# Three time steps per partition, Exp in place, and a first store in two parts: prefix log-sum-exp on one core

## The chip, the cores and the metric

The kernel runs on one NeuronCore of a Trainium2 chip. The metric is the device time of one execution in microseconds; lower is better. The kernel before takes 1265.46 us (median of 10 runs, 1264.6 to 1266.16).

## The reference

`x` is float32 of shape (4, 4096, 4128): four sequences of 4096 time steps, 4128 columns each. The output is the running log-sum-exp along time, kept per column:

```
out[:, 0, :] = x[:, 0, :]
for t in range(1, S):
    mx = np.maximum(out[:, t - 1, :], x[:, t, :])
    out[:, t, :] = mx + np.log(np.exp(out[:, t - 1, :] - mx) + np.exp(x[:, t, :] - mx))
```

This is the log of a prefix sum of exp(x), and that is how the kernel works: Exp, a prefix sum over time by matrix multiplication, Ln. 270.53 MB are read and 270.53 MB written.

## The kernel before

A tile holds 256 consecutive time steps of one sequence, all 4128 columns: partition p holds the R = 2 steps 2p and 2p+1, which lie side by side in DRAM, so a partition's run is 33,024 bytes. Tiles live in `xpool` (5 buffers). There are 64 of them, 16 per sequence, worked through in order of time.

The columns of a tile are taken in four chunks of 1024; a tail of 32 columns rides along with the last one. For a chunk, ScalarE writes Exp of both rows as fp16 into a buffer `et` (L111, four buffers). TensorE then forms the prefix sum in PSUM (`pt`, three buffers of two banks): `incl`, a triangle of ones with its diagonal, times the first rows, plus `excl`, the triangle without it, times the second rows, plus `pick` times the carry of the tile before (`head`). That is the sum up to each partition's first row; Ln of it goes into row 0 of the tile in place (L126). TensorE then adds `ident` times the second rows (`second`), and Ln of the result goes into row 1 (`close`). VectorE takes the last partitions of `pt` as the carry, as an fp16 value and an fp16 remainder (`keep`, L90 and L91). The tail has a small PSUM tile `qt` of its own and one Ln for both rows (L149).

Inside a tile the chunks are staggered by hand in `run`: while the Exp of chunk c is issued, row 0 of chunk c-1 and row 1 of chunk c-2 are finished. At the end of a tile everything drains before the next tile's first Exp.

Order of the transfers: all loads (L102) and stores (L153) are issued by the SP queue, in program order. Four loads are issued at the start; then comes, for each tile i, the load of tile i+3 (where there is one not yet issued) and the store of tile i. From tile 5 on a load reuses the buffer of an earlier tile and waits on SP until that tile's store has landed; the stores behind it wait as well. The instruction orders of the engines are fixed by the program (a manual schedule); a layer under it derives the semaphore waits from which tiles and columns each instruction reads and writes.

Of the kernel before, what the change touches and what calls it, by code (L numbers as in the profile page):

```python
# [7 lines left out]
FP32 = mybir.dt.float32  # L8
FP16 = mybir.dt.float16
ACT = mybir.ActivationFunctionType  # L10
P = 128
R = 2
CH = 1024
MM = 512
HI, LO = 96, 32
# [2 lines left out]
def _constants(nc, pool):  # L18


    def tri(base, name):
        t = pool.tile([P, P], FP16, name=name)
        nc.gpsimd.memset(t, 1.0)

        nc.gpsimd.affine_select(  # L25
            out=t, in_=t, pattern=[[1, P]], compare_op=mybir.AluOpType.is_ge,
            fill=0.0, base=base, channel_multiplier=-1,
        )
        return t

    def ones_where_zero(bases, step, name):
        t = pool.tile([P, P], FP16, name=name)
        nc.gpsimd.memset(t, 0.0)
        for base in bases:
            nc.gpsimd.affine_select(  # L35
                out=t, in_=t, pattern=[[step, P]], compare_op=mybir.AluOpType.not_equal,
                fill=1.0, base=base, channel_multiplier=1,
            )
        return t

    return (
        tri(0, "incl"),
        tri(-1, "excl"),
        ones_where_zero([0], -1, "ident"),
        ones_where_zero([-(HI + 31), -(LO + 31)], 0, "pick"),
    )


@with_exitstack
def kernel(  # L50
    ctx: ExitStack,
    tc: tile.TileContext,
    x: bass.AP,
    out: bass.AP,
):

    nc = tc.nc
    B, S, D = x.shape  # L60
    rows = P * R
    n_t = S // rows
    assert S % rows == 0
    n_main = D // CH
    tail = D - n_main * CH
    t0 = n_main * CH

    nc.scalar.preload_act_table_set("natural_log_exp_and_others")  # L68
    consts = ctx.enter_context(tc.tile_pool(name="consts", bufs=1))
    incl, excl, ident, pick = _constants(nc, consts)  # L70

    xpool = ctx.enter_context(tc.tile_pool(name="xpool", bufs=5))
    epool = ctx.enter_context(tc.tile_pool(name="epool", bufs=4))
    cpool = ctx.enter_context(tc.tile_pool(name="cpool", bufs=1))
    pmain = ctx.enter_context(tc.tile_pool(name="pmain", bufs=3, space=bass.MemoryType.PSUM))
    ptail = ctx.enter_context(tc.tile_pool(name="ptail", bufs=2, space=bass.MemoryType.PSUM))

    carry = [cpool.tile([P, CH], FP16, name=f"carry{c}") for c in range(n_main)]
    carry_t = cpool.tile([P, tail], FP16, name="carry_t")
    for t in (*carry, carry_t):  # L80
        nc.vector.memset(t, 0.0)  # L81

    ctx.enter_context(tc.manual_schedule())

    def mm(pt, w, rhs, start, stop):
        nc.tensor.matmul(pt, lhsT=w, rhs=rhs, start=start, stop=stop, skip_group_check=True)  # L86

    def keep(cr, pt):

        nc.vector.tensor_copy(cr[HI:HI + 32, :], pt[HI:HI + 32])  # L90
        nc.vector.tensor_tensor(  # L91
            out=cr[LO:LO + 32, :], in0=pt[HI:HI + 32], in1=cr[HI:HI + 32, :],
            op=mybir.AluOpType.subtract,
        )

    class Step:
        def __init__(self, b, k):
            self.first = k == 0
            self.xt = xpool.tile([P, R, D], FP32, name="xt")
            self.et, self.pt = {}, {}  # L100
            self.dram = lambda t: t[b, k * rows:(k + 1) * rows, :].rearrange("(p j) d -> p j d", j=R)
            nc.sync.dma_start(out=self.xt, in_=self.dram(x))  # L102

        def cols(self, c):
            return slice(c * CH, (c + 1) * CH if c + 1 < n_main else D)

        def exp(self, c):
            s = self.cols(c)
            w = s.stop - s.start
            et = epool.tile([P, R, CH + tail], FP16, name="et")  # L110
            nc.scalar.activation(et[:, :, :w], self.xt[:, :, s], ACT.Exp)  # L111
            self.et[c] = et

        def head(self, c):
            et = self.et[c]
            pt = self.pt[c] = pmain.tile([P, CH], FP32, name="pt")
            for s in range(0, CH, MM):
                mm(pt[:, s:s + MM], incl, et[:, 0, s:s + MM], True, False)
            for s in range(0, CH, MM):
                mm(pt[:, s:s + MM], excl, et[:, 1, s:s + MM], False, self.first)  # L120
            if not self.first:
                for s in range(0, CH, MM):
                    mm(pt[:, s:s + MM], pick, carry[c][:, s:s + MM], False, True)

        def ln(self, j, c):
            nc.scalar.activation(self.xt[:, j, c * CH:(c + 1) * CH], self.pt[c], ACT.Ln)  # L126

        def second(self, c):
            pt = self.pt[c]
            for s in range(0, CH, MM):  # L130
                mm(pt[:, s:s + MM], ident, self.et[c][:, 1, s:s + MM], False, True)

        def close(self, c):

            self.ln(1, c)
            keep(carry[c], self.pt[c])

        def tail_mm(self):
            et = self.et[n_main - 1]
            qt = self.qt = ptail.tile([P, R, tail], FP32, name="qt")  # L140
            e0, e1 = et[:, 0, CH:], et[:, 1, CH:]
            for j in range(R):
                mm(qt[:, j, :], incl, e0, j == 0, False)
                mm(qt[:, j, :], incl if j else excl, e1, False, self.first)
                if not self.first:
                    mm(qt[:, j, :], pick, carry_t, False, True)

        def ln_tail(self):
            nc.scalar.activation(self.xt[:, :, t0:D], self.qt, ACT.Ln)  # L149
            keep(carry_t, self.qt[:, 1, :])  # L150

        def store(self):
            nc.sync.dma_start(out=self.dram(out), in_=self.xt)  # L153

        def run(self):
            last = n_main - 1
            self.exp(0)
            self.head(0)
            for c in range(1, n_main):
                self.exp(c)  # L160
                self.head(c)
                if c == last:
                    self.tail_mm()
                self.ln(0, c - 1)
                self.second(c - 1)
                if c >= 2:
                    self.close(c - 2)
            self.ln(0, last)
            self.second(last)
            self.close(last - 1)  # L170
            self.ln_tail()
            self.close(last)
            self.store()

    work = [(b, k) for b in range(B) for k in range(n_t)]
    ahead = 3
    steps = []
    for i, (b, k) in enumerate(work):
        if i == 0:
            steps += [Step(*work[n]) for n in range(ahead)]  # L180
        if i + ahead < len(work):
            n = i + ahead
            steps.append(Step(*work[n]))
        steps[i].run()


# [28 lines left out]
```

The softmax here doesn't subtract the row's maximum and nothing guards it: scores larger than these inputs give would overflow.

## Time and profile before

| | |
|---|---|
| median of 10 runs | 1265.46 us |
| the profiled execution | 1264.59 us, span 1262.9 us |
| DMA queue of SP | 18,432 packets, busy 99.5% of 16 engines' span |
| ScalarE busy | 963.4 us (76%) |
| TensorE busy, weight loads | 667.4 us (53%), 242.4 us (19%) |
| VectorE busy | 655.8 us (52%) |
| load, from issue to landing | median 29.4 us |
| store, from issue to landing | median 38.6 us |
| one Ln of 128 x 1024 | 1028 ns |
| one Exp of 128 x 2048 | 1903 ns |

The share of a row is its busy time over the span of the profiled execution. A transfer of 4,128 KB runs on 16 DMA engines, eight descriptors (one per partition) and a completion on each. The time from issue to landing is longer than the transfer itself, because earlier transfers stand ahead of it on the same engines. The trace also keeps a record of each packet on the DMA engines, with its queue, size, start and duration; the queues 8 and 14 in it fetch instructions.

### The profile page before, as it was taken

How to read it: one execution, taken by the hardware profiler on the slowest of the kernel's cores; microseconds unless marked ns; L12 is line 12 of the kernel's file. 1: busy time of each engine (PE TensorE's matmuls, PEld its weight loads, DVE VectorE, ACT ScalarE, POOL GpSimd, SP SyncE). 2: the span in 40 equal slices, each digit the busy share in tenths (PEclk: the TensorE clock that was granted, in tenths of full speed). 3: DMA queues.
4: the chain of work that ended last, by engine and by line, in shares of the span. 5: the costliest groups of instructions: out<-in, count | busy, mean ns of one | idle time of the engine just before them, and what ended most of it. 6: DMA issues, size and time to landing. Idle time of an engine off the chain costs nothing.

```text
span 1262.9 us, 7025 instructions
## 1 busy us (share of the span) xinstructions
PE 667.4 (53%) x2392; PEld 242.4 (19%) x2392; DVE 655.8 (52%) x645; ACT 963.4 (76%) x833; POOL 2.2 (0%) x13
## 2 busy tenths in 40 slices
PE   2665655535455454554554555546545555455551
PEld 1222221212112121121111221212112121121220
DVE  3556655464454544545546455464564544645443
ACT  5888878778678787787877877777778777787772
POOL 0000000000000000000000000000000000000000
PEclk9778778787777777777777778767687677877776
DMA  9999999999999999999999999999999999999997
GB/s 402 417 433 429 433 430 434 429 431 432 434 430 434 433 431 432 432 434 433 434 430 433 432 434 433 434 433 431 433 432 431 432 434 434 433 434 434 431 433 335
DMA packets 18466, 541.51 MB, mean 429 GB/s; under 512 B 2048, under 2 KB 2048, under 8 KB 2048
## 3 DMA queue, kind: packets, MB, share of 16 engines
q1 hardware_dynamic: 18432, 541.07, 99.5%
q8 instruction: 19, 0.31, 0.1%
q14 instruction: 15, 0.12, 0.0%
HBM read 270.53 MB, written 270.53 MB: 428 GB/s over the span
## 4 chain that ended last, share of the span: by engine, by line
DMA 88%; ACT 1%; PE 1%; SPq 1%; DVE 1%; issue 0%; ACTq 0%
DMA out_dram<-xt 83%; DMA xt<-in_x_dram 5%; PE pt L86 1%; SPq L102 1%; ACT xt L126 1%; ACT et L111 0%; DVE carry L90 0%; DVE carry L91 0%; SPq L153 0%; DVE carry_t L90 0%; DVE carry_t L91 0%; ACTq L126 0%
## 5 line engine op out<-in xcount | busy, mean ns | idle before, releaser
L90 DVE CAST carry<-pt 32x1024 f16<-32x1024 f32 x256 | 314.9, 1230 | 574.1 <-ACT xt L126 570.8
L126 ACT ACTIVATE xt<-pt 128x1024 f32<-128x1024 f32 x512 | 504.4, 1028 | 126.1 <-PE pt L86 65.3
L111 ACT ACTIVATE et<-xt 128x2048 f16<-128x2048 f32 (+1 forms) x256 | 485.4, 1920 | 149.3 <-DMA xt<-in_x_dram 149.3
L86 PE MATMUL pt<-et,incl 128*128 128x512 f16 x512 | 211.0, 504 | 546.1 <-ACT et L111 373.7
L91 DVE TENSOR_TENSOR carry<-pt,carry 32x1024 f16<-32x1024 f32 x256 | 314.0, 1226 | 8.8
L86 PE MATMUL pt<-et,excl 128*128 128x512 f16 x512 | 211.6, 505 | 0.0
L86 PEld LDWEIGHTS <-incl 128*128 128x128 f16 x704 | 69.2, 111 | 683.8 <-issue 640.6
L86 PE MATMUL pt<-carry,pick 128*128 128x512 f16 x480 | 194.9, 497 | 0.0
L86 PE MATMUL pt<-et,ident 128*128 128x512 f16 x512 | 178.3, 435 | 24.8 <-ACT xt L126 24.8
L86 PEld LDWEIGHTS <-excl 128*128 128x128 f16 x576 | 71.3, 124 | 116.6 <-issue 84.7
L86 PEld LDWEIGHTS <-pick 128*128 128x128 f16 x600 | 69.5, 118 | 94.7 <-issue 66.9
L86 PEld LDWEIGHTS <-ident 128*128 128x128 f16 x512 | 49.4, 106 | 100.3 <-issue 73.7
L86 PE MATMUL qt<-et,incl 128*128 128x32 f16 x192 | 20.0, 192 | 0.0
L86 PE MATMUL qt<-carry_t,pick 128*128 128x32 f16 x120 | 15.6, 182 | 0.0
L149 ACT ACTIVATE xt<-qt 128x64 f32<-128x64 f32 x64 | 14.5, 227 | 0.0
L90 DVE CAST carry_t<-qt 32x32 f16<-32x32 f32 x64 | 12.6, 197 | 2.0
L91 DVE TENSOR_TENSOR carry_t<-qt,carry_t 32x32 f16<-32x32 f32 x64 | 12.4, 193 | 2.2
L86 PE MATMUL qt<-et,excl 128*128 128x32 f16 x64 | 11.7, 183 | 0.0
L81 DVE MEMSET carry<- 128x512 uint32 x4 | 1.9, 485 | 1.1 <-PEq L199 1.0
L68 ACT ACT_TABLE_LOAD x1 | 1.3, 1283 | 0.8 <-PEq L199 0.8
L35 POOL TENSOR_SCALAR_AFFINE_SELECT pick<-pick 128x128 f16<-128x128 f16 x2 | 0.6, 292 | 0.1
L25 POOL TENSOR_SCALAR_AFFINE_SELECT excl<-excl 128x128 f16<-128x128 f16 x1 | 0.3, 293 | 0.0
(11 smaller groups left out, 1.9 us busy)
## 6 DMA issues: line engine op xcount, KB each, us to landing
xt<-in_x_dram SPq DMA_DIRECT2D x64, 4128.0 KB, 29.4
out_dram<-xt SPq DMA_DIRECT2D x64, 4128.0 KB, 38.6
```

Source lines behind the costliest of these rows:

```text
L25: nc.gpsimd.affine_select(out=t, in_=t, pattern=[[1, P]], compare_op=mybir.AluOpType.is_ge, fill=0.0, base=base, channel_multiplier=-1,)
L35: nc.gpsimd.affine_select(out=t, in_=t, pattern=[[step, P]], compare_op=mybir.AluOpType.not_equal, fill=1.0, base=base, channel_multiplier=1,)
L68: nc.scalar.preload_act_table_set("natural_log_exp_and_others")
L81: nc.vector.memset(t, 0.0)
L86: nc.tensor.matmul(pt, lhsT=w, rhs=rhs, start=start, stop=stop, skip_group_check=True)
L90: nc.vector.tensor_copy(cr[HI:HI + 32, :], pt[HI:HI + 32])
L91: nc.vector.tensor_tensor(out=cr[LO:LO + 32, :], in0=pt[HI:HI + 32], in1=cr[HI:HI + 32, :], op=mybir.AluOpType.subtract,)
L102: nc.sync.dma_start(out=self.xt, in_=self.dram(x))
L111: nc.scalar.activation(et[:, :, :w], self.xt[:, :, s], ACT.Exp)
L126: nc.scalar.activation(self.xt[:, j, c * CH:(c + 1) * CH], self.pt[c], ACT.Ln)
L149: nc.scalar.activation(self.xt[:, :, t0:D], self.qt, ACT.Ln)
```

## The change

R becomes 3: partition p of a tile holds three consecutive time steps, 49,536 bytes. 4096 steps are 32 blocks of 128, so a sequence has ten tiles of three rows and one of two; in the first sequence the two-row tile comes first, in the others last. There are 44 tiles, and `xpool` has four buffers of three-row size. Matrix products go on as before with one more stage: after row 0, `ident` times the next row is added twice.

There is no `et` buffer. The tile is also seen as fp16 (`half`), and Exp writes its fp16 result over the first half of the bytes of the same columns; the Ln of a row later overwrites them with float32.

The chunks of all tiles form one stream. In pass g ScalarE does the third row of chunk g-2, the second of g-1, the first of g, and then Exp of chunk g+2, across the ends of tiles.

Four loads are issued first. A tile's store is issued after the last row of its last chunk, and then the load that is three tiles ahead. The first tile is stored in two parts: as soon as its first chunk of 1024 columns is done, these columns are stored by a DMA on ScalarE's queue (`store_apart`); the rest follows on SP.

```diff
-R = 2
+R = 3
...
-    xpool = ctx.enter_context(tc.tile_pool(name="xpool", bufs=5))
-    epool = ctx.enter_context(tc.tile_pool(name="epool", bufs=4))
+    bufs = 4
+    xpool = ctx.enter_context(tc.tile_pool(name="xpool", bufs=bufs))
...
+        def load(self):
+            full = xpool.tile([P, R, D], FP32, name="xt")
+            self.xt = full[:, :self.r, :]
+            self.half = self.xt.bitcast(FP16)
             nc.sync.dma_start(out=self.xt, in_=self.dram(x))
...
-        def exp(self, c):
-            s = self.cols(c)
-            w = s.stop - s.start
-            et = epool.tile([P, R, CH + tail], FP16, name="et")
-            nc.scalar.activation(et[:, :, :w], self.xt[:, :, s], ACT.Exp)
-            self.et[c] = et
...
+        def store(self):
+            a = self.apart
+            nc.sync.dma_start(out=self.dram(out)[:, :, a:], in_=self.xt[:, :, a:])
+
+        def store_apart(self):
+
+            a = self.apart = CH
+            nc.scalar.dma_start(out=self.dram(out)[:, :, :a], in_=self.xt[:, :, :a])
...
+        def exp(self):
+            c0, w = self.c * CH, self.w
+            nc.scalar.activation(
+                self.t.half[:, :, 2 * c0:2 * c0 + w], self.t.xt[:, :, c0:c0 + w], ACT.Exp,
+            )
+
+        def head(self):
+            t = self.t
+            pt = self.pt = pmain.tile([P, CH], FP32, name="pt")
+            for j in range(t.r):
                 for s in range(0, CH, MM):
...
+                    mm(pt[:, s:s + MM], excl if j else incl, self.e(j, s, s + MM), start=j == 0)
+            if not t.first:
+                for s in range(0, CH, MM):
+                    mm(pt[:, s:s + MM], pick, carry[self.c][:, s:s + MM])
+            if self.c == last:
+                self.tail_head()
...
+        def stage(self, j):
+
+            t, c, pt = self.t, self.c, self.pt
+            nc.scalar.activation(t.xt[:, j, c * CH:(c + 1) * CH], pt, ACT.Ln)
+            if j + 1 < t.r:
+                for s in range(0, CH, MM):
+                    mm(pt[:, s:s + MM], ident, self.e(j + 1, s, s + MM), stop=j + 2 == t.r)
+                if c == last and j == 0:
+                    nc.scalar.activation(t.xt[:, :, t0:D], self.qt, ACT.Ln)
+                    keep(carry_t, self.qt[:, t.r - 1, :])
+            else:
+                keep(carry[c], pt)
...
+    chunks = [Chunk(s, c) for s in steps for c in range(n_main)]
+    ahead = bufs - 1
+    for s in steps[:bufs]:
+        s.load()
+    stored = 0
+    chunks[0].exp()
+    chunks[1].exp()
+    chunks[0].head()
+    for g in range(len(chunks) + R - 1):
+        for d in range(R - 1, -1, -1):
+            if 0 <= g - d < len(chunks) and d < chunks[g - d].t.r:
+                k = chunks[g - d]
+                k.stage(d)
+                if k is chunks[0] and d + 1 == k.t.r:
+                    k.t.store_apart()
+                if k.c == last and d + 1 == k.t.r:
+                    k.t.store()
+                    if bufs <= stored + ahead < len(steps):
+                        steps[stored + ahead].load()
+                    stored += 1
+        if g + 2 < len(chunks):
+            chunks[g + 2].exp()
+        if g + 1 < len(chunks):
+            chunks[g + 1].head()
```

Unchanged are `keep`, the constants and the carry tiles. The tail's products are written for a variable number of rows (`tail_head`): one `incl` product of row i feeds all rows from i on, one `excl` product the rows before it.

## The prediction

> **What bounds the kernel now.** I read the page's slices, queues and chain first, then the waits of ScalarE and of the SP queue, then the timeline of the start and the end.
>
> ```profile
> span 1262.9 us, 7025 instructions
> DMA  9999999999999999999999999999999999999997
> GB/s 402 417 433 429 433 430 434 429 431 432 434 430 434 433 431 432 432 434 433 434 430 433 432 434 433 434 433 431 433 432 431 432 434 434 433 434 434 431 433 335
> q1 hardware_dynamic: 18432, 541.07, 99.5%
> DMA 88%; ACT 1%; PE 1%; SPq 1%; DVE 1%; issue 0%; ACTq 0%
> ...
> ACT et L111 <- DMA xt<-in_x_dram: 149.3, 56, 10.9
> ...
> SPq L102 <- DMA out_dram<-xt: 1083.8, 59, 19.4
> ```
>
> The DMA engines are busy 99.5% of the span. 541.07 MB must move, and no slice is above 434 GB/s. The chain is DMA; ScalarE, the busiest compute engine, waits for loads 56 times (149.3 us). So the kernel is bound by transfers, and only three things can change its time: cost per byte on the rings, stretches in which the rings are empty, and the two ends.
>
> The packet records give the cost per byte. The 16,384 data descriptors of 33,024 B have a median of 1222 ns, the 8,192 B descriptors of the instruction queue 309 ns. The line through both is 7.8 ns plus bytes/27.2 per ns. Eight descriptors make one engine's share of a tile: 9.8 us a transfer, 19.6 us a load and store, which is the distance of two loads on SP (1134.27 to 1153.94). Per engine: 1024 x 1.222 + 128 completion descriptors x 0.009 = 1252.5 us. First packet at 1.82 us, last ended at 1261.57: 1259.75 us, so the slowest engine has 7.3 us on top. Of this 0.6 lies in the very first descriptors and 1.2 at the first switch to writing (39 us); the rest is small switches and instruction fetches. At the end no ring runs dry: the last store is issued at 1239.64 and there are transfers ahead of it until about 1251.
>
> Start of the kernel before:
>
> ```profile
> 12.96 3.71 ACT L111 ACTIVATE et<-xt 128x2048 f16<-128x2048 f32 x2 [10.88 <-DMA xt<-in_x_dram]
> 16.89 1.02 ACT L126 ACTIVATE xt<-pt 128x1024 f32<-128x1024 f32 x1 [0.22 <-PE pt L86]
> 17.81 1.90 ACT L111 ACTIVATE et<-xt 128x2048 f16<-128x2048 f32 x1
> 19.61 1.93 ACT L126 ACTIVATE xt<-pt 128x1024 f32<-128x1024 f32 x2
> 21.41 1.97 ACT L111 ACTIVATE et<-xt 128x2112 f16<-128x2112 f32 x1
> ...
> 29.11 0.34 SPq L153 DMA_DIRECT2D out_dram<-xt  x1
> ...
> 46.01 0.34 SPq L153 DMA_DIRECT2D out_dram<-xt  x1
> ```
>
> Four loads keep the rings full until 39 us; the first two stores are queued at 29 and 46 us, before they are needed. This cover is what the change touches.
>
> **What the Trainium skill says.** "DMA: Bandwidth & Descriptors", section "Where 436 GB/s comes from", puts the ceiling of the SBUF ports at 435.2 GB/s; the trace's 434 agrees. So longer runs can win only the 7.8 ns. The same page, "Queues, rings and completion order", says that each engine takes turns between queue rows, a whole packet at a time, typically 9 to 17 descriptors. The trace disagrees for this kernel's transfers: of some thirty descriptors that another queue slipped in (at 321.459, 352.843 and 490.504 us, for example), each starts 3 or 4 ns after a data descriptor of the main queue, several with 2 to 4.5 us to the next completion. So the turn passes after one large descriptor. The main queue's next descriptor then takes 1.35 to 1.79 us, mean about 1.61, instead of 1.22.
>
> **The change part by part**
>
> 1. Runs of 49,536 B. Per engine 640 descriptors at 1829 ns (the line above), 56 of 33,024 B at 1222, the divided first store (16 at 158 ns, 16 at 464), 89 completions: 1170.6 + 68.4 + 2.5 + 7.4 + 0.8 = 1249.7 us, against 1252.5: -2.8. The extra of the slowest engine should shrink a little with 89 transfers for 128: 6 for 7.3, another -1.3. If long runs gain nothing (1833 ns, in proportion), the first sum gains nothing.
>
> 2. Compute. Per three-row tile ScalarE has 12 Ln at about 1.0 us (1.94 for two), 4 Exp at 2.85 us (1.5 x 1903 ns) and a tail: 23.8 us. TensorE has 48 matmuls of 512 columns at 0.41 us (211 us for 512) and short ones: 21 us. A load and a store need 2 x 14.63 = 29.3 us. So both stay beside the DMA. The Exp in place removes the et buffers; its added waits on ScalarE's own earlier instructions lie in the same slack. VectorE's carry work falls by a third, and was hidden. A carry takes 2.46 us (1.23 + 1.23), then the next head of the same PSUM buffer takes 8 matmuls, 3.3 to 4 us; ScalarE has two Ln, an Exp and two more Ln in that time, about 7 us. Cost 0; a miss of 1 us a chunk (24 + 4 us a tile) still fits into 29.3.
>
> 3. Buffers. Four three-row tiles for five two-row ones. A load follows the store of the tile before on SP and waits for the store before that one, as now; between that store's end and this load lie a load and a store, 29 us of queued work. Store n is ready about 16 us after load n+1 has landed and is needed 29 us after it. Cost 0.
>
> 4. The end. After the last load three stores remain, 14.6 + 14.6 + 9.8 us. The last is ready about 22 us of ScalarE work plus 4 or 5 of TensorE latency after that load, needed after 29.3: cost 0, at most 3.
>
> 5. The store put apart. This decides. In the emitted order of the changed kernel ScalarE runs
>
> ```
> L169 Activation xt<-pt 128x1024 [waits PE_49,Activation_49]
> L123 DMACopy out_dram<-xt 256x1x1024 [waits Activation_49]
> L169 Activation xt<-pt 128x1024 [waits PE_49]
> L135 Activation xt<-xt 128x2x1056 [waits DMAHW2_49]
> ```
>
> Loads 0 to 3 raise the semaphores 0, 1, 3 and 4; number 2 is raised by the store apart, and the load that reuses the first tile waits for it too. So the Exp of the first tile's fourth chunk waits until the store of the first chunk has *landed*. (It overwrites other columns of the tile; the wait is there all the same.) Behind it on ScalarE stand every Ln and Exp to come, and for these wait TensorE, VectorE and all stores on SP, with the loads queued behind them.
>
> How long? The Ln before the store ends at 20.6 as in the rows above; issue, and the first packet 1.0 us later (as for the first load, 0.81 to 1.82): 21.7. Each engine has 16 descriptors of 4,096 B for it, while loads 1 to 3 fill the SP ring with 24 of 1829 ns, 19 of them left at 21.7. Turn about, one for one, a turn is 1.829 + 0.158 + x, where x is what the interruption costs: 0 to 0.39 (the 1.61 above). The trace has no such mix; I take 0.2. W = 21.7 + 16 x 2.19 + 1 for the landing = 57.7 us; 54.5 to 62 at the bounds. In the order before, this Exp ran at 21.41.
>
> From W to the first tile's store: this Exp 1.97, five Ln 5.0, two Exp of the next tile 5.7, tail 0.23: 12.9. To the second tile's: 13 Ln, five Exp (14.4), a tail: 27.6, plus 1 of latency. So that store starts at W + 42.5 with its issue. The rings have work until then for 1.8 + 0.6 + 9.8 + 43.9 (loads) + 2.5 + 7.4 (stores) + 1.2 (switch) = 67.2, and load 5 stands behind this store on SP. Loss = W - 25 = 33 us, in two gaps: 8 us before the first store, about 19 before the second, and the interrupted turns. Nothing gives it back, since the DMA is full from there on.
>
> Sum on the profiled execution (1264.59 us, span 1262.9): -4.1 + 32.7 gives 1293.2, span 1291.5. The median of the runs shown, 1265.46, is 0.87 above that execution, so 1294.
>
> **The rivals**
> - *Short turn* (not slower): the 16 small descriptors drain in one packet, as the page has it, or share the ring finely. W = 21.7 + 1.8 + 2.5 + 1 = 27; the next tile lands only at about 30, which hides most of the wait, and the second store loses 1 to 2 us. 1265.5 - 4 + 1 = 1262. For it: the page's 9 to 17, and that the trace shows only single small-queue descriptors, never a row of them. Against: the switches in the middle of transfers. It decides for W up to about 29, where loss and gain meet.
> - *Several a turn*: 4 small descriptors each time, W about 34, loss 9: 1270. In general 1264 to 1283. Nothing in the trace speaks for it but the gap between the other two.
> - *Long runs gain nothing and the end runs dry*: up to +3 + 3 on either case; it only widens them.
>
> **How the numbers follow.** One for one 0.72 (own range 1286 to 1301), several a turn 0.09, short turn 0.19 (1259 to 1264). Predicted 1294; from 1264, which takes in "several a turn" and leaves the short turn out, to 1301. A measurement can tell about 0.2% (2.5 us) from no change. Faster 0.18, within 0.2% 0.03, slower 0.79.
>
> **What would show it.** Right: ScalarE idle some 30 to 38 us from 22 us on, released by the store apart; first two full stores near 71 and 98 us; DMA tenths down in slices 3 and 4 only; 1.83 us descriptors and slices at 433 or 434 after. Wrong: the fourth Exp near 28 us, no dent in the DMA row, and a span under 1261; then the turn passes several small descriptors. If slices later than the fifth dip too, point 2 or 3 is wrong.

## The result, and the profile after

The changed kernel takes 1294.28 us (median of 8 runs, 1293.73 to 1294.55) where the kernel before, run beside it, takes 1265.41 (28 runs): a ratio of 1.0227, 95% interval 1.0218 to 1.0236. Slower by 29 us. The profiled execution has a span of 1292.6 us.

From its page: the span, the DMA rows in 40 slices of 32.3 us, the two data queues (packets, MB, share of the engines' span), and the shares of the chain that ended last.

```profile
span 1292.6 us, 6166 instructions
...
DMA  9729999999999999999999999999999999999998
GB/s 409 343 123 393 431 428 438 431 429 436 434 430 435 434 434 427 440 431 426 441 425 441 428 437 431 431 433 437 429 437 428 437 431 431 435 434 428 436 424 347
...
q1 hardware_dynamic: 12800, 540.02, 96.9%
q10 hardware_dynamic: 272, 1.05, 0.2%
...
DMA 69%; ACT 21%; PE 6%; issue 2%; DVE 1%; SPq 0%; ACTq 0%
```

The DMA row has one dent, in the second and third slice, and is full from the fifth on, up to a short gap before the end that is taken up below. The loss stands in the first 97 us: by the packet records the engines are idle there for 32.3 us as a mean, and for 1.9 us in the first run below, which leaves the store apart out. ScalarE has 21% of the chain where it had 1%, but that is no sign of the loss: without the store apart it is 19%. The two waits of ScalarE for transfers (total us, times, longest us):

```profile
ACT xt L135 <- DMA xt<-in_x_dram: 244.4, 41, 11.0
...
ACT xt L135 <- DMA out_dram<-xt: 33.1, 1, 33.1
```

The first is the old wait for loads, which costs nothing here (247.0 us in the run without the store apart, which is the fastest): it means that compute is ahead. The second is new, one single wait of 33.1 us, for a *store*. The timeline of ScalarE shows where it stands, and that of SP what it does (start, duration, engine and line, operation, count, idle time before it; 68.91 is two stores merged, the second is issued at 95.8):

```profile
17.74 1.90 ACT L135 ACTIVATE xt<-xt 128x2048 f16<-128x2048 f32 x1
19.67 1.02 ACT L169 ACTIVATE xt<-pt 128x1024 f32<-128x1024 f32 x1
20.73 0.65 ACTq L123 DMA_DIRECT2D out_dram<-xt  x1
21.42 1.02 ACT L169 ACTIVATE xt<-pt 128x1024 f32<-128x1024 f32 x1 [0.73 <-ACT xt L169]
55.59 1.96 ACT L135 ACTIVATE xt<-xt 128x2112 f16<-128x2112 f32 x1 [33.14 <-DMA out_dram<-xt]
...
68.91 27.28 SPq L118 DMA_DIRECT2D out_dram<-xt  x2
96.30 0.37 SPq L114 DMA_DIRECT2D xt<-in_x_dram  x1
```

The Exp of the first tile's fourth chunk (128 x 2112) runs at 55.59 instead of about 22. The first store on SP follows at 68.91, the second at 95.8, and the fifth load only behind it, at 96.30. The rings have nothing to do in between, as the same stretches in both kernels show (length, busy time and count of each engine, TensorE clock, DMA share, GB/s); first after, then before:

```profile
55.00:69.00 14.00, 6.47 (x19) 2.38 (x19) 5.38 (x7) 12.28 (x10) 0.00 (x0) 0.58 0.24 103
69.00:96.00 27.00, 18.61 (x64) 6.76 (x64) 10.29 (x11) 25.87 (x20) 0.00 (x0) 0.81 0.28 118
```

```profile
55.00:69.00 14.00, 8.44 (x28) 2.96 (x29) 10.07 (x10) 12.14 (x11) 0.00 (x0) 0.63 0.99 423
69.00:96.00 27.00, 16.21 (x66) 5.95 (x64) 16.40 (x16) 24.75 (x24) 0.00 (x0) 0.81 1.00 431
```

A DMA share of 0.24 over 14 us and 0.28 over 27 us: 10.6 + 19.4 = 30 us of empty rings, as a mean over the engines.

### The profile page after: what moved, and what is told of

Same layout as the page of the kernel before. It is cut to its first block, busy times and chain, and to the rows that moved or that the text cites. A ratio compares the mean times of both kernels' runs of the same rounds, so it can differ in the third digit from the quotient of the medians.

```text
span 1292.6 us, 6166 instructions
## 1 busy us (share of the span) xinstructions
PE 689.2 (53%) x2268; PEld 237.1 (18%) x2268; DVE 451.4 (35%) x445; ACT 947.2 (73%) x733; POOL 2.2 (0%) x13
## 4 chain that ended last, share of the span: by engine, by line
DMA 69%; ACT 21%; PE 6%; issue 2%; DVE 1%; SPq 0%; ACTq 0%
DMA xt<-in_x_dram 64%; ACT xt L135 11%; ACT xt L169 9%; PE pt L88 6%; DMA out_dram<-xt 5%; DVE carry L92 0%; DVE carry L93 0%; ACT xt L174 0%; SPq L118 0%; ACTq L240 0%; ACTq L135 0%; SPq L114 0%; PE qt L88 0%
## 5 line engine op out<-in xcount | busy, mean ns | idle before, releaser
L135 ACT ACTIVATE xt<-xt 128x3072 f16<-128x3072 f32 (+3 forms) x176 | 478.5, 2719 | 277.5 <-DMA xt<-in_x_dram 244.4
L88 PE MATMUL pt<-xt,ident 128*128 128x512 f16 x672 | 253.2, 474 | 561.8 <-ACT xt L169 561.3
L92 DVE CAST carry<-pt 32x1024 f16<-32x1024 f32 x176 | 216.4, 1230 | 792.4 <-ACT xt L169 792.2
L88 PE MATMUL pt<-xt,excl 128*128 128x512 f16 x672 | 246.0, 502 | 0.0
L93 DVE TENSOR_TENSOR carry<-pt,carry 32x1024 f16<-32x1024 f32 x176 | 215.9, 1226 | 6.1
L88 PE MATMUL pt<-xt,incl 128*128 128x512 f16 x352 | 152.8, 528 | 23.4 <-ACT xt L135 14.9
L88 PEld LDWEIGHTS <-excl 128*128 128x128 f16 x756 | 92.4, 124 | 141.4 <-issue 108.6
L88 PE MATMUL pt<-carry,pick 128*128 128x512 f16 x320 | 108.9, 426 | 0.0
L88 PEld LDWEIGHTS <-incl 128*128 128x128 f16 x480 | 45.8, 112 | 131.6 <-DVE carry L93 95.3
L88 PEld LDWEIGHTS <-pick 128*128 128x128 f16 x360 | 40.3, 112 | 56.4 <-issue 33.2
## 6 DMA issues: line engine op xcount, KB each, us to landing
out_dram<-xt ACTq DMA_DIRECT2D x1, 1024.0 KB, 34.8
```

What stands on the lines that cost most here:

```text
L93: nc.vector.tensor_tensor(out=cr[LO:LO + 32, :], in0=pt[HI:HI + 32], in1=cr[HI:HI + 32, :], op=mybir.AluOpType.subtract,)
L135: nc.scalar.activation(self.t.half[:, :, 2 * c0:2 * c0 + w], self.t.xt[:, :, c0:c0 + w], ACT.Exp,)
```

## Experiments

Each is an edit of the changed kernel unless said otherwise. Ratios are against the kernel before, run on the same chip.

**Leaving the store apart out**

```diff
-                if k is chunks[0] and d + 1 == k.t.r:
-                    k.t.store_apart()
```

> The store apart is left out; the first tile is stored whole, all else as in the changed kernel. Theory (the fourth Exp waits for the store apart): ScalarE no longer waits at 22 us, the second tile's store is issued at about 65 us, before the rings are empty at 67, so no gap at the start: 1294.3 - 33 = 1261.5 us, within 1259 to 1264, faster than before by about 0.3%. Rival (three rows, one buffer fewer and the long stream cost the time, and the store apart only sits in the same place): still above 1285, with dents in the DMA row at the start or later.

Measured: 1262.77 us, ratio 0.9981 (0.9973 to 0.9989). The DMA row, and the timelines of ScalarE and SP in this run:

```profile
DMA  9999999999999999999999999999999999999998
...
19.83 2.00 ACT L169 ACTIVATE xt<-pt 128x1024 f32<-128x1024 f32 x2
21.73 1.96 ACT L135 ACTIVATE xt<-xt 128x2112 f16<-128x2112 f32 x1
...
63.70 0.34 SPq L118 DMA_DIRECT2D out_dram<-xt  x1
68.65 0.34 SPq L114 DMA_DIRECT2D xt<-in_x_dram  x1
```

The fourth Exp runs at 21.73 without a wait, and the second store is issued at 63.70, while the first is still on the rings. All of the loss is the store apart, and what remains of the change is a gain of 2.6 us.

**The same store, behind the Exp**

```diff
         if g + 2 < len(chunks):
             chunks[g + 2].exp()
+        if g == 1:
+            chunks[0].t.store_apart()
```

(and the call in the stage loop removed)

> The same store apart, on the same queue and of the same size, but placed behind the fourth Exp instead of ahead of it. Theory: nothing on ScalarE waits for its landing any more; the 16 turns of small descriptors stay and cost 0 to 4 us of ring time: 1261 to 1266 us. Rival (the mixing of two queues itself, 272 small descriptors between loads, costs the time): about as slow as the changed kernel, above 1285. The packet records should show the small descriptors spread over 30 us as before.

Measured: 1263.02 us, ratio 0.9982 (0.9975 to 0.9989). Timeline of ScalarE:

```profile
21.76 1.96 ACT L135 ACTIVATE xt<-xt 128x2112 f16<-128x2112 f32 x1
23.75 0.65 ACTq L123 DMA_DIRECT2D out_dram<-xt  x1
24.45 1.94 ACT L169 ACTIVATE xt<-pt 128x1024 f32<-128x1024 f32 x2 [0.73 <-ACT xt L135]
```

The same 256 small descriptors pass through the same load stream, and the time is 0.25 us over that without a store apart, which the intervals of the two ratios don't tell apart. Two instructions further down in ScalarE's order, behind one Ln and the Exp, the store costs 31 us less. So the traffic is harmless and the wait is everything.

**Half the partitions**

```diff
-            nc.scalar.dma_start(out=self.dram(out)[:, :, :a], in_=self.xt[:, :, :a])
+            nc.scalar.dma_start(out=self.dram(out)[:64, :, :a], in_=self.xt[:64, :, :a])
```

(the other 64 partitions of these columns by one more store on SP)

> The store apart covers 64 partitions instead of 128 (8 small descriptors per engine instead of 16); the other 64 are stored with the rest on SP. Theory (one small descriptor per turn, loss = end of the wait minus a constant): the fourth Exp starts 8 turns of 1.98 us earlier, at 39.8 instead of 55.6 us, and the time falls by the same 16 us: 1278 us, within 1275 to 1281. Rival (the wait lasts until the loads are through, whatever the store's size): the Exp at about 55 us and 1292 to 1295.

**Half the columns**

```diff
-            a = self.apart = CH
+            a = self.apart = 512
```

> The store apart covers 512 columns instead of 1024: as many descriptors, 16 per engine, of 2,048 B instead of 4,096 B. Theory (a turn is paid per descriptor, and the load's descriptor is nearly all of it): 16 x 0.075 us shorter, the Exp at 54.4 us, 1293 us, within 1291 to 1295. Rival (the queues share by bytes): half the wait, the Exp near 39 us and about 1278.

Measured, each with the ratio: half the partitions 1279.92 us, 1.0116 (1.0101 to 1.0131); half the columns 1292.73 us, 1.0218 (1.0201 to 1.0235). The fourth Exp, half the partitions first, then half the columns:

```profile
41.82 1.97 ACT L137 ACTIVATE xt<-xt 128x2112 f16<-128x2112 f32 x1 [19.15 <-DMA out_dram<-xt]
```

```profile
54.60 1.96 ACT L135 ACTIVATE xt<-xt 128x2112 f16<-128x2112 f32 x1 [31.93 <-DMA out_dram<-xt]
```

Both stores carry half the bytes. With half the descriptors the wait ends 13.8 us earlier, with half the size of each only 1.0 us. The packet records of the changed kernel show the same: in most steps of 1.98 us (1.829 for a load's descriptor, 0.159 for a small one) exactly 16 small descriptors start, which fits one on each of 16 engines (a record doesn't name its engine). Only at about 27 and 43 us twice as many start, so the 16 descriptors of an engine took 14 turns; the completion took one more. That is also why half the partitions saved seven turns and not the eight that were expected (the Exp at 41.8 us, not 39.8). So the store pays about a turn per descriptor, and here a turn lasted little longer than the other queue's descriptor.

**The store apart on SP**

```diff
-            nc.scalar.dma_start(out=self.dram(out)[:, :, :a], in_=self.xt[:, :, :a])
+            nc.sync.dma_start(out=self.dram(out)[:, :, :a], in_=self.xt[:, :, :a])
```

> The store apart is issued on SP's queue, so it stands behind the four loads on the same rings, and no turns are taken between queues. Theory (only the end of the wait matters, however it comes about): it lands when the loads are through, 56.1 + 2.5 + 1.2 for the first switch + 0.5 = 60.3 us; the Exp then, 4.7 us later than in the changed kernel, and 1294.3 + 4.7 = 1299 us, within 1296 to 1301. Rival (the loss comes from two queues sharing the engines): without the sharing the time falls below 1290.

Measured: 1299.31 us, ratio 1.0268 (1.0251 to 1.0286). ScalarE:

```profile
61.05 1.96 ACT L135 ACTIVATE xt<-xt 128x2112 f16<-128x2112 f32 x1 [39.01 <-DMA out_dram<-xt]
```

Without any turns between queues the wait is longer still, since the store now stands behind all the loads. Put together:

| run | fourth Exp starts, us (W) | time, us | time - W |
|---|---|---|---|
| half the partitions | 41.82 | 1279.92 | 1238.10 |
| half the columns | 54.60 | 1292.73 | 1238.13 |
| the changed kernel | 55.59 | 1294.28 | 1238.69 |
| store apart on SP | 61.05 | 1299.31 | 1238.26 |

Over 19 us of W the difference moves by 0.6 us: each microsecond of wait is one microsecond of time. If this line is carried on below the W that were measured, it meets the time of the kernel before, 1265.4, at W = 27, and the time without the store apart, 1262.8, at W = 24.5.

**Row 0 alone, at the old place**

```diff
-            nc.scalar.dma_start(out=self.dram(out)[:, :, :a], in_=self.xt[:, :, :a])
+            nc.scalar.dma_start(out=self.dram(out)[:, 0, :a], in_=self.xt[:, 0, :a])
```

(row 1 of these columns by one more store on SP)

> The store apart covers row 0 of the first chunk only (all partitions, 128 descriptors of 4,096 B on ScalarE's queue, issued at the same place, ahead of the fourth Exp); row 1 of it goes with the rest on SP. In the emitted order the fourth Exp has no wait for it. Theory (the wait is derived from address extents: the store of two rows spans the bytes between its rows, where the Exp writes, the store of one row doesn't): the Exp runs at about 22 us and the time is that without the store apart, 1261 to 1265 us. Rival (what holds ScalarE is the DMA that it issued itself, not a wait that the program names): the Exp at about 40 us and 1278.

Measured: 1263.32 us, ratio 0.9984 (0.9978 to 0.9991); the Exp runs at once:

```profile
19.95 0.38 ACTq L125 DMA_DIRECT2D out_dram<-xt  x1
20.92 1.02 ACT L171 ACTIVATE xt<-pt 128x1024 f32<-128x1024 f32 x1
21.84 1.96 ACT L137 ACTIVATE xt<-xt 128x2112 f16<-128x2112 f32 x1
```

So a store on ScalarE's queue ahead of the Exp doesn't hold it as such. In bytes of a partition, the two-row store covers 0 to 4,095 and 16,512 to 20,607; the Exp writes 12,288 to 14,399 and 28,800 to 30,911. They share no byte, but the spans from first to last overlap. With row 0 alone, the store's span ends at 4,095. This fits a wait derived from spans where the two sides see the tile in different types (float32 and fp16); the Ln that follow write other columns of the same tile as float32, and in the emitted order they show no such wait (the line behind the store in the order that the prediction shows). How the layer decides is not on record, and no run has the same store with both sides in one type, so the rule stays an inference. What the runs show is the wait and what removes it.

**The kernel before with the store apart**

```diff
+                if c == 2 and self is steps[0]:
+                    nc.scalar.dma_start(out=self.dram(out)[:, :, :CH], in_=self.xt[:, :, :CH])
```

(and the first tile's other store from column 1024 on)

> The kernel before, with only the store apart added: the first tile's first 1024 columns go on ScalarE's queue behind row 1 of chunk 0. There Exp writes to buffers of its own, so nothing of the tile is written at the place that the store's wait covered. Theory: no wait, the fourth Exp at about 22 us, 16 turns in the load stream: 1265 to 1268 us. Rival (any store on ScalarE's queue in the load phase holds the kernel up): 1285 or more.

Measured: 1265.61 us, ratio 1.0003 (0.9994 to 1.0011). ScalarE goes on as soon as the issue is done:

```profile
21.73 0.65 ACTq L170 DMA_DIRECT2D out_dram<-xt  x1
22.43 1.96 ACT L111 ACTIVATE et<-xt 128x2112 f16<-128x2112 f32 x1 [0.72 <-ACT xt L126]
```

The store apart is harmless where Exp has a buffer of its own; in these runs it stalls only together with Exp in place.

**Two rows per tile in the new stream, no store apart**

```diff
-R = 3
+R = 2
...
-    bufs = 4
+    bufs = 6
```

> Two rows per tile again (33,024 B runs, 64 tiles, six buffers, six loads up front), but with Exp in place and the stream of chunks, and no store apart. Theory (all that the change can win is the fixed 7.8 ns of each descriptor and the completions, 2.8 us): 2.8 us above the run with three rows without the store apart, so 1265.5 us, the time of the kernel before. Rival (the stream and the Exp in place win it, by keeping stores earlier): as fast as three rows, 1262 to 1263.

Measured: 1264.38 us, ratio 0.9992 (0.9983 to 1.0000). Between the two expectations: three rows, with four buffers for six, are worth 1.6 us in time, the rest of the change about 1 us, which the interval doesn't clear of nothing. In the packet records the transfers of the two queues keep an engine busy for 1256.8 us in the kernel before, 1256.2 here and 1254.1 with three rows and no store apart (means of the 16). By these most of the gain belongs to the longer runs.

**Filling the gap at the end**

Without the store apart the rings still run dry once, at 1228 to 1235 us, before the last but one store. By the packet records that is 4.2 us as a mean over the engines (the expectation has 3.7).

```diff
                 k.stage(d)
+                if k.t in steps[-2:] and k.c == 1 and d + 1 == k.t.r:
+                    k.t.store_apart()
```

(`store_apart` on SP, with 2048 columns; the one of the first tile left out)

> As the run without the store apart, and the last two tiles are stored in two parts each on SP, their first 2048 columns as soon as these are done, so that the rings don't run dry at 1228 to 1235 us, where 3.7 us of mean idle time stood. Theory A (that mean gap is time lost): 1262.8 - 3.7 = 1259 us. Theory B (one engine was busy nearly all through the gap, so only the engines that were ahead stood idle, and the slowest engine sets the end): the gap moves to the very end, where the engines finish at different times, and the gain is at most 1 us: 1261.8 to 1263.3.

Measured: 1263.54 us, ratio 0.9986 (0.9980 to 0.9993); 0.8 us more than without, with intervals that overlap. The gap is gone, and 4.5 us of mean idle time stand at the very end instead: engines finish between 1253.0 and 1260.1 us, where they finished between 1259.1 and 1259.5 with the gap. One engine is some 7 us behind the foremost, and it was busy through nearly all of the gap (its last completion before it comes at 1234.9, the first engine's at 1227.9). The others only waited for it earlier. The divided stores have a price: 80 descriptors of 309 and 315 ns on each engine for 16 of 1829 and 1222 ns, an estimate of 0.55 us. Even without it the time would be 1263.0, far from the 1259 of a gap that is lost time. So next to no time lay in the gap, and the fastest version here is the one with whole stores.

## Why the prediction was right

The forecast, 1294 us, the sign and the mechanism held: one wait of ScalarE for the store apart, and one small descriptor a turn for most of it; the exact agreement with 1294.28 is partly luck, as the terms show.

1. *Runs of 49,536 B.* The line through two sizes gave 1829, 158 and 464 ns; the records show medians of 1829, 159 and 465. The gain of 2.8 us for the longer runs came to 1.6 in time (2.1 in the engines' busy time), run against run with two rows. The further 1.3 us for fewer switches did not come: the extra time of the large descriptors was 4.3 us an engine before and 4.6 without the store apart. The whole -4.1 was -2.6. (The instruction descriptors from which the prediction read the length of a turn start 3 or 4 ns ahead of the end of a data descriptor's record, not behind it; the reading that they stand between two data descriptors isn't touched by that.)

2. *Compute* cost nothing, as said. Exp of 3072 took 2.77 us instead of the 2.85 worked out.

3. *Buffers* cost nothing: the DMA row is full from the fifth slice on.

4. *The end.* Here a step failed, without a cost. The prediction looked at the last store, which was in time (about 23.4 us after the last load, 26 to 27 expected), and not at the one before it: that came when the engines that were ahead had run dry, 3.9 us of mean idle time. The run with the filled gap showed that this is next to no time lost.

5. *The store apart.* W was 55.6 us, not 57.7, out of several errors that in part cancel. The first small descriptors started at 25.0 us, and on most engines at about 27, not at 21.7: after the end of the issue at 21.4, the time of two to three large descriptors went by first. Against that, interruptions lengthened nothing (the large descriptors next to the small ones still took 1829 ns, where 0.2 us each was taken; 3.3 us in 16 turns), and two turns passed two small descriptors. From W to the issue of the two stores: 13.3 and 40.2 us, worked out as 12.9 and 41.5. Because the turns were shorter, the rings ran dry earlier than the prediction had it, and the dent stands in slices 2 and 3, not in 3 and 4 as its sign said. The loss as a whole is 31.5 us (1294.28 - 1262.77), worked out as 33. Loss and gain were both put about 1.5 us too large, and they cancel.

Two sums of the prediction do not come out of its own terms. With 0.39 us for an interruption the upper bound of W is 60.7, not 62. And gaps of 8 and about 19 us with 16 interruptions of 0.2 make 30, not 33; the measured gaps were 10 and 20. The 33 comes from the other sum, W - 25, and that one is close to the line above, W - 24.5.

The rival with several descriptors a turn is ruled out here by the pace of 1.98 us and by the two halves. So is the short turn: the Trainium skill's page "DMA: Bandwidth & Descriptors", section "Queues, rings and completion order", has an engine drain a whole packet of typically 9 to 17 descriptors from one ring before it switches, and here never more than two small ones went by. The point from which the sign turns, put at W of about 29, comes out at 27 if the line is carried on.

## What to carry to other kernels

- Before moving or adding a store, read in the emitted order which waits the compute instructions behind it have got. A transfer that should run beside the work can end up in front of it, for bytes that it doesn't touch; two instructions further down were worth 31 us here.
- On rings that another queue kept busy, the time of a small transfer followed the number of its descriptors per engine times the neighbour's descriptor, not its bytes over the bandwidth: 1 MB took 34.8 us from issue to landing, half of it 33.6 us in as many descriptors and 20.8 us in half as many.
- A mean idle time of DMA engines need not be a loss: the gap of 4.2 us was worth next to nothing, since one engine was busy through nearly all of it. Look at the slowest.

## What was not expected of the hardware

The engines drift apart. In the kernel before, the first of the 16 ends its last transfer at 1253.2 us and the last at 1261.6, with equal bytes on each. A short pause near the end lines them up again without making the program longer. Which engine is behind, and why, is open.

An issue of a DMA takes time by its shape, and what counted here was the number of runs in a partition: 0.65 us on ScalarE for a store of two rows of 4,096 B in each of 128 partitions, 0.64 us with 64 partitions or with rows of 2,048 B, 0.64 us for the same two-row store on SP, and 0.38 us on ScalarE for one row of 4,096 B in each partition. With the last stores divided on SP, stores of two and three rows took 0.53 to 0.64 us. A whole tile with one run in a partition took SP 0.33 to 0.40 us in most issues.
